# A decoder layer on one core: the top-k threshold of sparse attention found by steered counts and a max of eight instead of a bitwise search

## The chip, the core and the metric

The kernel runs on one core of one Trainium2 chip. Its engines run side by side, each with its own queue in program order: TensorE (PE, matmuls; PEld its weight loads), VectorE (DVE), ScalarE (ACT), GpSimd (POOL) and SyncE (SP, which issues all transfers here). The metric is the device time of one execution in microseconds; lower is better.

## The reference, cut to what matters

One layer on 1024 tokens of width 1024: an input norm, a joint projection, sliding-window attention (A) beside sparse attention (B), an output projection, cross-attention over 256 memory tokens, and an MLP. The change is in how B chooses its keys:

```python
dots = einsum('bqhd,bsd->bqhs', iqb, ik) * (IDX_DIM ** -0.5)   # 8 index heads of 64
score = einsum('bqh,bqhs->bqs', iwb, relu(dots))
score = where(causal, score, NEG_INF)
_, idx = lax.top_k(score, 256)        # per row; ties: the lower index wins
...                                   # attention over these 256 keys alone
```

A row with at most 256 keys (blocks 0 and 1 of 128 rows) keeps them all. So only blocks n = 2 to 7, with 384 to 1024 keys, need a choice.

## The kernel before, in words

All matmuls split fp32 operands into a high and a low part. Rows lie on the 128 partitions in eight blocks. `index_scores` (L599) leaves the scores of block n in `sc` as 128 x (n+1)*128 fp32.

The threshold of a row is its 256th largest score. It is searched bit by bit on an integer key of the score: `to_keys` (L590) turns the upper 16 bits into an ordered int16 key, and a loop at L706 does the same with the lower 16. `search` (L692) runs 15 rounds on the upper halves. After that the lower halves are masked to the rows' equal upper halves (L709 to L712), and 16 more rounds run on them. In a round each block has one look: a pass over the keys that counts those at or above a trial bound, and two 128x1 steps that set or clear the bit. Blocks 5, 4, 3 and 2 are counted on DVE (`Counter`, L649, by `count`, L583), blocks 7 and 6 on ACT as a sum of signs (`Signer`, L670). Then the key is put together as fp32 (L714 to L727), and for each block five passes of DVE (L733 to L737) turn `sc` into an additive mask: 0 for a chosen key and -1e30 for another, with a running sum that lets only the needed number of equal scores through. Sparse attention (`dsa_unit`, L838) adds that mask at L860.

Meanwhile PE works on `fill` (L490 to L550), a list of 60 units of other work: 18 projections of queries and keys (weights split by POOL, results copied by ACT at L393 and split by POOL at L395, L396), the latent keys, and the keys, values and output products of the memory tokens (`mem_k`, `mem_v`, `mem_vo`; some of their weights are split by DVE at L158 and L161, and DVE finishes values at L466). Weights come through four raw tiles (`wr`), loaded by SP at L152 and freed by the splits. Every unit is traced after the whole search:

```python
    behind["PE"] = [Pace(score_mm, 45, 1.2)]
    for unit, *args in fill:
        unit(*args)
```

A planner orders each engine's queue: by the order of tracing where it can, by its own forecast of when operands are ready where not. Attention (L884) follows, units of A and B in turn.

Of the kernel before, what the change touches and what calls it, by code (L numbers as in the profile page):

```python
# [21 lines left out]
P = 128  # L22
KT = D // P
NB = T // P
# [3 lines left out]
NEG = -1e30  # L28
ALPHA = 2.0 ** 0.25
BUCKETS = 32  # L30
NOSYNC = mybir.DependencyInfo(mybir.DependencyClass.NoSync, mybir.DependencyReason.DATA)


# [1 line left out]
def kernel(ctx: ExitStack, tc: tile.TileContext, x, mem, ln_emb_g, ln_emb_b, w_in, b_in,  # L35
# [25 lines left out]
    def f(ap):  # L61
        return ap.bitcast(F32)
# [28 lines left out]
    class Pace:  # L91

        def __init__(self, lead, start, rate):
            self.lead, self.at, self.rate = lead, start, rate
# [179 lines left out]
        ACT.activation(xin[tb], xin[tb], AF.Identity, scale=r, bias=nm)  # L274


    TW = 328
    TC = ((0, 640, 128), (128, 1280, 128), (256, 1920, 72))
    btok = p0.tile([P, TW], F32)
# [58 lines left out]
    for tb in range(NB):  # L338
        tok_cols(tb)
    bias_rows()  # L340
    st0.close()
    HALVES = ((0, 512), (512, 512))

# [8 lines left out]
    def kdup(pl, src, *names):  # L352
        kk = [place(pl, n, [P, T], F32R) for n in names]
        for hl in range(2):
            for e in range(2):
                SP.dma_start(f(kk[hl])[e * 64:e * 64 + 64], src[hl])
        return kk
# [191 lines left out]
    for at, u in zip((13, 11, 10, 9, 8, 6, 5), [(open_attention,)] + [(first_loads, i) for i in range(6)]):  # L549
        fill.insert(len(fill) - at, u)  # L550

    ik = kdup(p1, ik_d, ("ikh",), ("ikl",))
    cm = p1.tile([P, P], F32, name="cm")
    DVE.memset(cm, 0.0)
# [1 line left out]

    ring = [0]
    score_mm = []
    hi_k = {}
    HI = {7: (3, 0), 3: (7, 1024), 6: (4, 0), 4: (6, 896), 5: (2, 0), 2: (5, 768)}  # L560
    NQ = NB - 2
    cnt0, neg, flip, low, least, T_hi, base, need, t_lo = (
        p1.tile([P, NQ], F32, name=nm) for nm in ("cnt0", "neg", "flip", "low", "least", "T_hi", "base", "need", "t_lo"))

    def halves(n, which, dt=U16):
        return sc.bitcast(dt)[:, which + 2 * SCO[n]:2 * (SCO[n] + (n + 1) * P):2]

    def hi_half(n):
        mate, o = HI[n]
        if (n, mate) not in hi_k:  # L570
            hi_k[n, mate] = hi_k[mate, n] = p1.tile([P, 1536], I16, name="hi_k", tag="qs", bufs=4)
        hi_k[n] = hi_k[n, mate][:, o:o + (n + 1) * P]
        return hi_k[n]

    def col(t, n):
        return t[:, n - 2:n - 1]

    junk = {}

    def new_junk():  # L580
        junk["v"] = p1.tile([P, 1024], BF, name="junk", tag="r", bufs=3)

    def count(key, c, o, op=OP.is_ge):  # L583
        DVE.tensor_scalar(junk["v"][:, :key.shape[-1]], key, c, None, op0=op, op1=OP.add, accum_out=o)

    def to_keys(n):  # L590
        new_junk()
        count(halves(n, 1, I16), 0.0, col(cnt0, n))
        DVE.tensor_scalar(col(neg, n), col(cnt0, n), float(TOPK), -1.0, op0=OP.is_ge, op1=OP.add)
        DVE.tensor_scalar(col(flip, n), col(neg, n), 2.0, 1.0, op0=OP.mult, op1=OP.add)
        POOL.tensor_scalar(hi_half(n), halves(n, 1, I16), col(flip, n), col(neg, n), op0=OP.mult, op1=OP.add)
        DVE.tensor_scalar(col(least, n), col(neg, n), col(cnt0, n), float(TOPK), op0=OP.mult, op1=OP.add)
        DVE.tensor_scalar(col(low, n), col(neg, n), -65535.0, None, op0=OP.mult)

    def index_scores(j, qs):  # L599
        for e in range(2):  # L600
            h = 2 * j + e
            for n in (2, 4, 6, 3, 5, 7):
# [15 lines left out]
                else:  # L618
                    DVE.scalar_tensor_tensor(s, r[:, :w], iw, s, op0=OP.mult, op1=OP.add)
                if h == 7:  # L620
                    to_keys(n)

    ahead = None
    for j in range(4):
# [5 lines left out]
        ahead = (j, qs)  # L630
    index_scores(*ahead)

    SIGN = (NB - 1, NB - 2)
    lo_k = {}
    for tag, bufs, ns in (("ikh", 1, (7, 6)), ("ikl", 1, (5, 4, 3)), ("qs", 4, (2,))):
        t = p1.tile([P, sum(n + 1 for n in ns) * P], U16, name="lo_k", tag=tag, bufs=bufs)
        o = 0
        for n in ns:  # L640
            lo_k[n] = t[:, o:o + (n + 1) * P]
            o += (n + 1) * P
    new_junk()
    junk_a = p1.tile([P, 1024], BF, name="junk_a", tag="r", bufs=3)

    def srow(n):
        return sc[:, SCO[n]:SCO[n] + (n + 1) * P]

    class Counter:  # L649

        def __init__(self, n, key, least, out, bits):
            self.n, self.key, self.least, self.out, self.bits = n, key, least, out, bits
            self.c = self.small("c")
            DVE.memset(self.c, float(1 << bits - 1))

        def small(self, nm):
            return p1.tile([P, 1], F32, name=nm + str(self.n), bufs=2)

        def look(self):
            self.got = self.small("n")  # L660
            count(self.key, self.c, self.got)

        def move(self, b):
            u = self.small("u")
            DVE.tensor_scalar(u, self.got, self.least, float(1 << b), op0=OP.is_ge, op1=OP.mult)
            o = self.small("c") if b else self.out
            DVE.tensor_scalar(o, u, self.c, -float(1 << b) / 2 if b else -1.0, op0=OP.add, op1=OP.add)
            self.c = o

    class Signer(Counter):  # L670

        def __init__(self, n, key, least, out, bits):
            self.n, self.key, self.out, self.bits = n, key, out, bits
            self.c, self.least = self.small("c"), self.small("l")
            DVE.memset(self.c, 0.5 - (1 << bits - 1))
            DVE.tensor_scalar(self.least, least, -2.0, float((n + 1) * P + 1), op0=OP.mult, op1=OP.add)

        def look(self):
            self.got = self.small("n")
            ACT.activation(junk_a[:, :self.key.shape[-1]], self.key, AF.Sign, bias=self.c, accum_out=self.got)  # L680

        def move(self, b):
            u = self.small("u")
            ACT.activation(u, self.got, AF.Sign, bias=self.least)
            if b:
                o = self.small("c")
                ACT.activation(o, u, AF.Identity, scale=-float(1 << b) / 2, bias=self.c)
                self.c = o
            else:
                DVE.tensor_scalar(self.out, u, 0.5, self.c, op0=OP.mult, op1=OP.subtract)  # L690

    def search(keys, least, out, bits):  # L692
        every = [(Signer if n in SIGN else Counter)(n, keys[n], col(least, n), col(out, n), bits) for n in range(NB - 1, 1, -1)]
        last = None
        for b in range(bits - 1, -1, -1):
            for s in every:
                s.look()
                if isinstance(s, Signer):
                    s.move(b)
                    continue  # L700
                if last is not None:
                    last[0].move(last[1])
                last = s, b
        last[0].move(last[1])

    for n in range(2, NB):  # L706
        POOL.tensor_scalar(lo_k[n], halves(n, 0), col(flip, n), col(low, n), op0=OP.mult, op1=OP.add)
    search(hi_k, least, T_hi, 15)
    for n in range(NB - 1, 1, -1):  # L709
        count(hi_k[n], col(T_hi, n), col(base, n), OP.is_gt)  # L710
        DVE.scalar_tensor_tensor(lo_k[n], hi_k[n], col(T_hi, n), lo_k[n], op0=OP.is_equal, op1=OP.mult)
        DVE.tensor_scalar(col(need, n), col(base, n), -1.0, col(least, n), op0=OP.mult, op1=OP.add)  # L712
    search(lo_k, need, t_lo, 16)
    thr = p1.tile([P, NQ], I32)  # L714
    hi_i = p1.tile([P, NQ], I32)
    lo = p1.tile([P, NQ], F32)
    DVE.tensor_tensor(out=lo, in0=t_lo, in1=flip, op=OP.mult)
    DVE.tensor_tensor(out=thr, in0=lo, in1=low, op=OP.add)
    DVE.tensor_tensor(out=lo, in0=T_hi, in1=flip, op=OP.mult)
    DVE.tensor_tensor(out=lo, in0=lo, in1=neg, op=OP.add)  # L720
    DVE.tensor_scalar(hi_i, lo, 65536.0, None, op0=OP.mult)
    DVE.tensor_tensor(out=thr, in0=thr, in1=hi_i, op=OP.bitwise_or)
    ngt = p1.tile([P, NQ], F32)
    for n in range(2, NB):
        count(lo_k[n], col(t_lo, n), col(ngt, n), OP.is_gt)
    DVE.tensor_tensor(out=ngt, in0=ngt, in1=need, op=OP.subtract)
    DVE.tensor_scalar(ngt, ngt, -NEG, None, op0=OP.mult)  # L727
    for n in range(2, NB):
        w = (n + 1) * P
        s = srow(n)  # L730
        t = f(thr[:, n - 2:n - 1])
        e, pre, le = (p1.tile([P, 1024], F32, name="r", bufs=3) for _ in range(3))
        DVE.tensor_scalar(e[:, :w], s, t, -NEG, op0=OP.is_equal, op1=OP.mult)  # L733
        DVE.tensor_tensor_scan(pre[:, :w], e[:, :w], e[:, :w], ngt[:, n - 2:n - 1], OP.add, OP.bypass)
        DVE.tensor_scalar(le[:, :w], s, t, NEG, op0=OP.is_le, op1=OP.mult)
        DVE.scalar_tensor_tensor(e[:, :w], pre[:, :w], -0.5 * NEG, e[:, :w], op0=OP.is_le, op1=OP.mult)
        DVE.tensor_tensor(out=s, in0=e[:, :w], in1=le[:, :w], op=OP.add)  # L737

    behind["PE"] = [Pace(score_mm, 45, 1.2)]
    for unit, *args in fill:  # L740
        unit(*args)
    behind.clear()
    s1.close()
# [676 lines left out]
```

## Time and profile before

| | us |
|---|---|
| median of 3 runs | 1579.77 (1577.89 to 1583.2) |
| the profiled execution | 1573.87 |
| its span | 1572.0 |
| PE / DVE / POOL / ACT busy | 1449.3 / 1165.3 / 847.4 / 798.3 |
| mean granted TensorE clock | 0.967 of full |

Busy time adds up instructions, so a PE at half its clock is busy longer with the same work; the granted clock has to be read beside it. The scores are done at about 161 us from the span's start; the last mask row ends at 384.7.

### The profile page before, as it was taken

The page shows a single profiled execution, that of the slowest core. Times are in us where ns is not written, and L with a number is a line of the kernel's source. Part 1 is how long each engine was busy: PE and PEld are TensorE (multiplying, and loading weights), DVE is VectorE, ACT ScalarE, POOL GpSimd, SP SyncE. Part 2 cuts the span into 40 slices and gives each one's busy share as a digit, 9 for nine tenths or more (in the row PEclk, how much of TensorE's full clock was granted, in tenths as well). Part 3 has the DMA queues.
Part 4 walks back from the last instruction along what each step waited for, and adds up shares of the span by engine and source line. Part 5 has one row for each costly group of instructions (what it writes and reads, how often), then busy time and mean ns, then how long its engine had stood idle before and what let it go on. Part 6 is the DMA issues. An engine that isn't in the chain of part 4 may idle for free. (4 is left out here: it accounts for less than half of the span.)

```text
span 1572.0 us, 22293 instructions
## 1 busy us (share of the span) xinstructions
PE 1449.3 (92%) x7190; PEld 1208.9 (77%) x7190; DVE 1165.3 (74%) x2442; ACT 798.3 (51%) x1665; POOL 847.4 (54%) x753
## 2 busy tenths in 40 slices
PE   5989998785998999899999979999999999999887
PEld 4877776765897987688888758888888887888666
DVE  8639899969687868985263495575544799988857
ACT  6336677664787864235334154545455444444422
POOL 6213856546556555666565585645445345454745
PEclk9999998986999999999999989999999999999999
DMA  6252445873748248633322133423333934420002
GB/s 218 75 161 68 135 134 154 247 237 93 211 137 241 94 154 267 185 103 105 101 82 84 42 102 121 138 103 129 113 106 100 395 110 134 145 70 1 27 32 103
DMA packets 139907, 206.63 MB, mean 131 GB/s; under 512 B 18055, under 2 KB 83086, under 8 KB 139790
## 3 DMA queue, kind: packets, MB, share of 16 engines
q1 hardware_dynamic: 139790, 205.21, 41.4%
q8 instruction: 57, 0.93, 0.3%
q14 instruction: 60, 0.49, 0.1%
HBM read 151.66 MB, written 52.45 MB: 130 GB/s over the span
## 5 line engine op out<-in xcount | busy, mean ns | idle before, releaser
L86 PE MATMUL b<-a,wh 128*128 128x512 f32 x1072 | 300.2, 402 | 8.8 <-DVE a L1075 8.1
L161 POOL TENSOR_TENSOR wl<-wr,wh 128x512 fp32r<-128x512 f32 x158 | 228.5, 1466 | 145.8 <-ACT wh L160 137.4
L86 PE MATMUL b<-wl,wh 128*128 128x512 f32 x1192 | 278.1, 393 | 13.5 <-POOL wl L1089 13.3
L86 PEld LDWEIGHTS b<-wl,wh 128*128 128x128 f32 x1192 | 224.9, 189 | 63.9 <-POOL wl L1089 16.3
L86 PEld LDWEIGHTS b<-a,wh 128*128 128x128 f32 x1072 | 203.5, 191 | 58.2 <-issue 8.9
L1089 POOL TENSOR_TENSOR wl<-a,wl 128x512 fp32r<-128x512 f32 x44 | 92.4, 2099 | 109.0 <-ACT wl L1088 99.2
L160 ACT ACTIVATE wh<-wr 128x512 fp32r<-128x512 f32 x136 | 81.1, 627 | 128.5 <-PE b L86 46.4
L1089 POOL TENSOR_TENSOR wh<-row,wh 128x512 fp32r<-128x512 f32 x72 | 98.1, 1368 | 88.5 <-ACT wh L1088 85.2
L86 PE MATMUL fill<-xT,wh 128*128 128x512 f32 (+1 forms) x416 | 126.8, 384 | 6.8 <-ACT wt L393 6.8
L86 PE MATMUL b<-wh,a 128*128 128x512 f32 (+1 forms) x416 | 122.5, 369 | 7.6 <-DVE a L761 5.6
L86 PE MATMUL b<-a,wl 128*128 128x512 f32 x400 | 123.0, 396 | 0.0
L1088 ACT ACTIVATE wh<-a 128x512 fp32r<-128x512 f32 x80 | 50.5, 631 | 111.5 <-PE b L86 82.0
L86 PEld LDWEIGHTS fill<-xT,wh 128*128 128x128 f32 x416 | 78.5, 195 | 23.0 <-ACT wt L393 8.3
L86 PEld LDWEIGHTS b<-wh,a 128*128 128x128 f32 x416 | 76.4, 191 | 22.8 <-DVE a L761 5.9
L1282 DVE TENSOR_TENSOR xr<-xr,b 128x512 f32<-128x512 f32 x132 | 81.5, 675 | 14.1 <-PE b L86 14.1
L86 PEld LDWEIGHTS b<-a,wl 128*128 128x128 f32 x400 | 75.0, 188 | 17.4
L86 PE MATMUL fill<-xT,wl 128*128 128x512 f32 (+1 forms) x208 | 79.8, 385 | 0.0
L1100 ACT ACTIVATE lt<-lt,colst 128x512 f32<-128x512 f32 x60 | 43.2, 722 | 68.1 <-DVE lt L1207 67.3
L86 PE MATMUL b<-wl,a 128*128 128x512 f32 (+1 forms) x208 | 76.2, 369 | 1.3 <-POOL wl L161 1.3
L1207 DVE TENSOR_TENSOR lt<-b,lt 128x512 f32<-128x512 f32 x80 | 53.3, 686 | 32.1 <-PE b L86 27.5
L769 DVE TENSOR_TENSOR PT<-tr,PT 128x512 fp32r<-128x512 f32 (+3 forms) x128 | 70.6, 576 | 8.7 <-ACT PT L768 8.4
L768 ACT ACTIVATE PT<-tr 128x512 fp32r<-128x512 f32 (+3 forms) x128 | 61.4, 507 | 25.1 <-PE tr L870 11.6
(327 smaller groups left out, 3664.8 us busy)
## 6 DMA issues: line engine op xcount, KB each, us to landing
row<-in_w_up_dram SPq DMA_DIRECT2D x32, 512.0 KB, 4.3
ff_d<-lt SPq DMA_DIRECT2D x28, 512.0 KB, 3.0
a<-in_w_down_dram SPq DMA_DIRECT2D x50, 256.0 KB, 5.2
a<-ff_d SPq DMA_DIRECT2D x46, 256.0 KB, 3.5
wr<-in_xa_wkv_dram SPq DMA_DIRECT2D x32, 256.0 KB, 4.0
wr<-in_w_o_dram SPq DMA_DIRECT2D x32, 256.0 KB, 3.2
wr<-in_xa_wq_dram SPq DMA_DIRECT2D x32, 256.0 KB, 2.7
wr<-vwo_d SPq DMA_DIRECT2D x32, 256.0 KB, 2.8
```

Source lines behind the costliest of these rows:

```text
L86: i = PE.matmul(o, a, b, start=start, stop=stop)
L160: ACT.activation(hs, raw, AF.Copy)
L161: lo[i % len(lo)].tensor_tensor(out=ls, in0=raw, in1=f(hs), op=OP.subtract)
L768: ACT.activation(PT[0], pt, AF.Copy)
L769: DVE.tensor_tensor(out=PT[1], in0=pt, in1=f(PT[0]), op=OP.subtract)
L1088: ACT.activation(hl[:, 0], raw, AF.Copy)
L1089: return lo.tensor_tensor(out=hl[:, 1], in0=raw, in1=f(hl[:, 0]), op=OP.subtract)
L1100: ACT.activation(c, src, AF.Relu, bias=colst[:, C_UP + col:C_UP + col + 1])
L1207: DVE.tensor_tensor(out=o, in0=a, in1=b, op=op)
L1282: DVE.tensor_tensor(out=xs, in0=xs, in1=p, op=op)
```

## The change

The integer keys and both searches go. In their place:

* `normal_bounds` (at the end of the first stage) works out, for each row's number of keys, where a normal distribution has its 251.5th largest value, and the slope there.
* When a block's scores are done, mean and deviation of the first 256 to 512 of them (`bn_stats`, `bn_aggr`, a power on POOL) give a first bound and a step per count.
* Eight rounds (`PULL`) of one look per block: the count of scores at or above the bound, compared with 251.5, moves the bound. The looks read the fp32 scores themselves; blocks 7 and 6 stay on ACT.
* A last count gives how many of the 256 are still below the bound (`need`). The scores at or above it are pushed down by 2^100, and a max-8 gives the eight largest of the rest: the `need`-th of them is the threshold.
* If any row has a `need` outside 1 to 8, all six blocks are settled by the old bitwise search, now on DVE alone and one step after another, behind a branch. The flag is gathered by a matmul of one column and read into a register of DVE.
* The mask rows keep their five passes. They are now traced, with the branch ahead of them, after the first 26 units of `fill` (`CUT`) and ahead of the other 34.

```diff
+PULL = (1.0, 0.8, 0.6, 0.9, 0.5, 0.3, 0.6, 0.25)
+WANT = TOPK - 4.5
...
+            w = min(512, n * P)
+            st, mv, sd = (self.own[:, a:b] for a, b in ((0, 6), (6, 8), (8, 9)))
+            DVE.bn_stats(st, srow(n)[:, :w])
+            DVE.bn_aggr(mv, st)
+            POOL.tensor_tensor(out=sd, in0=mv[:, 1:2], in1=half_up, op=OP.pow)
+            self.begin(mv, sd)
...
+        def begin(self, mv, sd):
+            self.c, g, self.rate = self.small("c"), self.own[:, 9:10], self.own[:, 12:20]
+            DVE.tensor_scalar(self.c, sd, col(zc, self.n), mv[:, 0:1], op0=OP.mult, op1=OP.add)
+            DVE.tensor_scalar(g, sd, col(gp, self.n), None, op0=OP.mult)
+            DVE.tensor_scalar(self.rate, pull, g, None, op0=OP.mult)
+        def look(self):
+            self.got = self.small("n")
+            s = srow(self.n)
+            DVE.tensor_scalar(junk["v"][:, :s.shape[-1]], s, self.c, None, op0=OP.is_ge, op1=OP.add, accum_out=self.got)
+
+        def move(self, i):
+            u, o = self.small("u"), self.small("c") if i < len(PULL) - 1 else col(bound, self.n)
+            DVE.tensor_scalar(u, self.got, WANT, self.rate[:, i:i + 1], op0=OP.subtract, op1=OP.mult)
+            DVE.tensor_scalar(o, u, self.c, None, op0=OP.add)
+            self.c = o
+
...
+    class Signer(Counter):
...
+        def look(self):
+            self.got = self.small("n")
+            s = srow(self.n)
+            ACT.activation(junk["a"][:, :s.shape[-1]], s, AF.Sign, bias=self.c, accum_out=self.got)
...
-                    to_keys(n)
+                    every[n] = (Signer if n in SIGN else Counter)(n)
...
-    search(hi_k, least, T_hi, 15)
...
-    search(lo_k, need, t_lo, 16)
...
+    for i in range(len(PULL)):
+        for n in range(NB - 1, 1, -1):
+            s = every[n]
+            s.look()
+            if n in SIGN:
+                s.move(i)
+                continue
+            if last is not None:
+                last[0].move(last[1])
...
+    for n in ORDER:
+        over[n] = p1.tile([P, 1024], BF, name="over", tag="qs", bufs=4)
+        DVE.tensor_scalar(over[n][:, :(n + 1) * P], srow(n), col(bound, n), None, op0=OP.is_ge, op1=OP.add, accum_out=col(base, n))
+    DVE.tensor_scalar(need, base, -1.0, float(TOPK), op0=OP.mult, op1=OP.add)
...
+    DVE.tensor_scalar(odd1, odd1, 16.0, None, op0=OP.is_gt)
+    ones = p1.tile([P, 1], F32, name="ones")
+    DVE.memset(ones, 1.0)
+    po = psum.tile([P, 512], F32, name="odd_rows", tag="mm", bufs=2)
+    PE.matmul(po[:1, :1], odd1, ones, start=True, stop=True)
+    some = p1.tile([1, 1], I32, name="some")
+    DVE.tensor_scalar(some, po[:1, :1], 1.0, None, op0=OP.min)
+    for i, n in enumerate(ORDER):
+        w = (n + 1) * P
+        v = p1.tile([P, 1024], F32, name="v", tag=("ikh", "ikl")[i % 2], bufs=1)
+        DVE.scalar_tensor_tensor(v[:, :w], over[n][:, :w], LAST, srow(n), op0=OP.mult, op1=OP.add)
+        DVE.max(m8[:, n - 2], v[:, :w])
...
+    def by_bits(key, most, least, o, bits, a, go, scratch):
+        go(DVE.memset(a[0], float(1 << bits - 1)))
         for b in range(bits - 1, -1, -1):
+            go(DVE.tensor_scalar(scratch, key, a[0], None, op0=OP.is_ge, op1=OP.add, accum_out=a[1]))
+            go(DVE.tensor_scalar(a[1], a[1], least, float(1 << b), op0=OP.is_ge, op1=OP.mult))
+            go(DVE.tensor_scalar(a[0], a[1], a[0], -float(1 << b) / 2 if b else -1.0, op0=OP.add, op1=OP.add))
...
+    def settle_all():
+        rest = nc.values_load(some, [mybir.EngineType.DVE], min_val=0, max_val=1)
+        with tc.tile_critical():
+            with nc.If(rest > 0):
+                for n in range(2, NB):
+                    settle(n)
...
-    for unit, *args in fill:
+    for unit, *args in fill[:CUT]:
+        unit(*args)
+    settle_all()
+    mask_rows()
+    for unit, *args in fill[CUT:]:
         unit(*args)
```

`settle(n)` makes the keys of one block, calls `by_bits` with 15 and with 16 bits, and puts the threshold together; each of its instructions waits for the one before. In `before`, the round loop and the classes are the removed ones named above.

## Rows read from the trace of the kernel before

**Rows 1.** The page, parts 1 and 2: busy time by engine; granted clock in 40 slices.

```profile
PE 1449.3 (92%) x7190; PEld 1208.9 (77%) x7190; DVE 1165.3 (74%) x2442; ACT 798.3 (51%) x1665; POOL 847.4 (54%) x753
PEclk9999998986999999999999989999999999999999
```

**Rows 2.** Windows: stretch, length, busy PE, PEld, DVE, ACT, POOL, clock, DMA share, GB/s.

```profile
160.00:230.00 70.00, 68.10 (x305) 55.28 (x304) 65.79 (x261) 53.71 (x136) 52.37 (x55) 1.00 0.50 139
230.00:354.00 124.00, 100.47 (x553) 86.05 (x551) 111.42 (x346) 83.80 (x198) 65.00 (x57) 0.88 0.67 210
354.00:400.00 46.00, 30.14 (x169) 26.97 (x170) 43.66 (x111) 21.74 (x65) 26.52 (x31) 0.74 0.34 86
400.00:1572.00 1172.00, 1118.73 (x5476) 928.17 (x5474) 829.30 (x1460) 559.62 (x1110) 644.24 (x546) 0.98 0.39 125
```

**Rows 3.** Waits of PE in 230 to 354: who, for whom, us, times, longest.

```profile
PE fill L86 <- DVE wl L161: 10.4, 7, 2.6
PE fill L86 <- ACT wt L393: 4.9, 1, 4.9
...
PE fill L86 <- DVE wh L158: 2.1, 3, 0.8
```

**Rows 4.** Timeline of DVE: start, us, operation; one round of four looks.

```profile
306.46 0.99 DVE L584 TENSOR_SCALAR_CACHE_REDUCE junk<-lo_k,c 128x768 bf16<-128x768 uint16 x1
...
307.39 0.20 DVE L665 TENSOR_SCALAR u<-n,need 128x1 f32<-128x1 f32 x1
307.52 0.20 DVE L667 TENSOR_SCALAR c<-u,c 128x1 f32<-128x1 f32 x1
...
310.37 1.00 DVE L584 TENSOR_SCALAR_CACHE_REDUCE junk<-lo_k,c 128x768 bf16<-128x768 uint16 x1
```

**Rows 5.** Waits of the SP queue in 200 to 360.

```profile
SPq L152 <- DVE wl L161: 24.1, 7, 5.5
```

**Rows 6.** Timeline of ACT: two looks of one block, and the second search's first.

```profile
205.71 1.06 ACT L680 ACTIVATE junk_a<-hi_k,c 128x896 bf16<-128x896 int16 x1
...
208.61 1.06 ACT L680 ACTIVATE junk_a<-hi_k,c 128x896 bf16<-128x896 int16 x1
...
234.74 1.15 ACT L680 ACTIVATE junk_a<-lo_k,c 128x1024 bf16<-128x1024 uint16 x1 [10.76 <-DVE lo_k L711]
```

**Rows 7.** Timeline of DVE: the last scores, and mask rows.

```profile
158.99 1.80 DVE L619 SCALAR_TENSOR_TENSOR sc<-r,iwt,sc 128x1024 f32<-128x1024 f32 x1
...
346.22 0.42 DVE L733 TENSOR_SCALAR r<-sc,thr 128x384 f32<-128x384 f32 x1
...
363.87 0.60 DVE L735 TENSOR_SCALAR r<-sc,thr 128x768 f32<-128x768 f32 x1
...
383.42 1.30 DVE L737 TENSOR_TENSOR sc<-r 128x1024 f32<-128x1024 f32 x1
```

**Rows 8.** Waits of PE in 354 to 400, the longest.

```profile
PE mm L86 <- DVE PT L769: 7.3, 1, 7.3
```

**Rows 9.** Groups of DVE by line in 346 to 385: busy us, mean ns, idle before.

```profile
L734 DVE TENSOR_TENSOR_SCAN r<-r,ngt 128x384 f32<-128x384 f32 (+5 forms) x6 | 10.2, 1704 | 0.1
L736 DVE SCALAR_TENSOR_TENSOR r<-r 128x384 f32<-128x384 f32 (+5 forms) x6 | 5.6, 940 | 0.0
L737 DVE TENSOR_TENSOR sc<-r 128x384 f32<-128x384 f32 (+5 forms) x6 | 5.5, 914 | 0.1
L733 DVE TENSOR_SCALAR r<-sc,thr 128x384 f32<-128x384 f32 (+5 forms) x6 | 5.0, 830 | 0.0
L735 DVE TENSOR_SCALAR r<-sc,thr 128x384 f32<-128x384 f32 (+5 forms) x6 | 4.5, 756 | 0.0
```

**Rows 10.** Line L584's instructions in 160 to 400: ns min/median/max, start, forms.

```profile
L584 DVE TENSOR_SCALAR_CACHE_REDUCE junk<-hi_k,T_hi x6: 603/936/1279, 232.2 to 240.4; 128x1024 bf16<-128x1024 int16 x1, 128x896 bf16<-128x896 int16 x1, 128x768 bf16<-128x768 int16 x1, 128x640 bf16<-128x640 int16 x1
```

**Rows 11.** Groups of DVE by form in 0 to 170: bn_stats of 512 columns.

```profile
L268 DVE BATCH_NORM_STATS2 bst<-wt 128x6 f32<-128x512 f32 x10 | 6.2, 663 | 2.5 <-DMA wt<-in_x_dram 2.5
```

**Rows 12.** The page, part 3: the instruction queue; packets, MB, share.

```profile
q8 instruction: 57, 0.93, 0.3%
```

More of the change, by code (lines that the diff above doesn't have):

```diff
@@ L30 @@
 BUCKETS = 32
+PULL = (1.0, 0.8, 0.6, 0.9, 0.5, 0.3, 0.6, 0.25)
+WANT = TOPK - 4.5
+LAST = -2.0 ** 100
 NOSYNC = mybir.DependencyInfo(mybir.DependencyClass.NoSync, mybir.DependencyReason.DATA)
@@ L340 @@
     bias_rows()
+    normal_bounds()
     st0.close()
@@ L550 @@
         fill.insert(len(fill) - at, u)
+    CUT = 26
     ik = kdup(p1, ik_d, ("ikh",), ("ikl",))
@@ L558, with srow @@
     score_mm = []
[L559 to L563, printed above, removed]
+    SIGN = (NB - 1, NB - 2)
+    bound, base, need, thr, ngt = (p1.tile([P, NQ], F32, name=nm) for nm in ("bound", "base", "need", "thr", "ngt"))
+    def srow(n):
+        return sc[:, SCO[n]:SCO[n] + (n + 1) * P]
@@ L565, in halves @@
     def halves(n, which, dt=U16):
         return sc.bitcast(dt)[:, which + 2 * SCO[n]:2 * (SCO[n] + (n + 1) * P):2]
[L568 to L573, printed above, removed]
     def col(t, n):
         return t[:, n - 2:n - 1]
-    junk = {}
-    def new_junk():
-        junk["v"] = p1.tile([P, 1024], BF, name="junk", tag="r", bufs=3)
@@ L583, in count, with __init__, small @@
[L583 to L597, printed above, removed]
+    class Counter:
+        def __init__(self, n):
+            self.n = n
+            self.own = p1.tile([P, 20], F32, name="own%d" % n)
+            self.way = p1.tile([P, 6], F32, name="way%d" % n)
+            self.turn = [0, 0, 0]
+            w = min(512, n * P)
[4 more added lines that the diff above has]
+            self.begin(mv, sd)
+        def small(self, nm):
+            k = "cnu".index(nm)
+            self.turn[k] += 1
+            i = 2 * k + self.turn[k] % 2
+            return self.way[:, i:i + 1]
+        def begin(self, mv, sd):
[12 more added lines that the diff above has]
+            self.c = o
@@ new lines, with begin, move @@
+    class Signer(Counter):
+        def begin(self, mv, sd):
+            self.c, g, self.rate = self.small("c"), self.own[:, 9:10], self.own[:, 12:20]
+            self.even = self.own[:, 10:11]
+            DVE.memset(self.even, (self.n + 1) * P - 2 * WANT)
+            DVE.tensor_scalar(self.c, sd, col(zn, self.n), mv[:, 0:1], op0=OP.mult, op1=OP.subtract)
+            DVE.tensor_scalar(g, sd, col(gn, self.n), None, op0=OP.mult)
+            DVE.tensor_scalar(self.rate, pull, g, None, op0=OP.mult)
+        def look(self):
+            self.got = self.small("n")
+            s = srow(self.n)
+            ACT.activation(junk["a"][:, :s.shape[-1]], s, AF.Sign, bias=self.c, accum_out=self.got)
+        def move(self, i):
+            u = self.small("u")
+            ACT.activation(u, self.got, AF.Identity, bias=self.even)
+            if i < len(PULL) - 1:
+                o = self.small("c")
+                ACT.activation(o, u, AF.Identity, scale=self.rate[:, i:i + 1], bias=self.c)
+                self.c = o
+            else:
+                v = self.own[:, 11:12]
+                DVE.tensor_scalar(v, u, self.rate[:, i:i + 1], self.c, op0=OP.mult, op1=OP.add)
+                DVE.tensor_scalar(col(bound, self.n), v, -1.0, None, op0=OP.mult)
@@ L599, in index_scores @@
+    junk, every = {}, {}
     def index_scores(j, qs):
@@ L631 @@
     index_scores(*ahead)
[L635 to L690, printed above, removed]
@@ L692, in search @@
-    def search(keys, least, out, bits):
-        every = [(Signer if n in SIGN else Counter)(n, keys[n], col(least, n), col(out, n), bits) for n in range(NB - 1, 1, -1)]
-        last = None
-        for b in range(bits - 1, -1, -1):
[L696 to L704, printed above, removed]
@@ L706 @@
-    for n in range(2, NB):
-        POOL.tensor_scalar(lo_k[n], halves(n, 0), col(flip, n), col(low, n), op0=OP.mult, op1=OP.add)
-    search(hi_k, least, T_hi, 15)
[L709 to L712, printed above, removed]
-    search(lo_k, need, t_lo, 16)
@@ L714 @@
[L714 to L728, printed above, removed]
-        w = (n + 1) * P
[L730 to L737, printed above, removed]
@@ L739 @@
-    behind["PE"] = [Pace(score_mm, 45, 1.2)]
-    for unit, *args in fill:
+    for k in ("v", "a"):
+        junk[k] = p1.tile([P, 1024], BF, name="junk", tag="r", bufs=3)
+    last = None
+    for i in range(len(PULL)):
[7 more added lines that the diff above has]
+                last[0].move(last[1])
+            last = s, i
+    last[0].move(last[1])
@@ new lines @@
+    m8 = p1.tile([P, NQ, 8], F32, name="m8")
+    ORDER = (2, 3, 4, 5, 6, 7)
+    over = {}
+    for n in ORDER:
+        over[n] = p1.tile([P, 1024], BF, name="over", tag="qs", bufs=4)
+        DVE.tensor_scalar(over[n][:, :(n + 1) * P], srow(n), col(bound, n), None, op0=OP.is_ge, op1=OP.add, accum_out=col(base, n))
+    DVE.tensor_scalar(need, base, -1.0, float(TOPK), op0=OP.mult, op1=OP.add)
+    odd, odd1 = p1.tile([P, NQ], F32, name="odd"), p1.tile([P, 1], F32, name="odd1")
+    DVE.tensor_scalar(odd, need, -4.5, None, op0=OP.add)
@@ new lines @@
+    DVE.tensor_tensor(out=odd, in0=odd, in1=odd, op=OP.mult)
+    DVE.tensor_reduce(out=odd1, in_=odd, op=OP.max, axis=AX.X)
+    DVE.tensor_scalar(odd1, odd1, 16.0, None, op0=OP.is_gt)
[5 more added lines that the diff above has]
+    DVE.tensor_scalar(some, po[:1, :1], 1.0, None, op0=OP.min)
@@ new lines, with each @@
+    for i, n in enumerate(ORDER):
[3 more added lines that the diff above has]
+        DVE.max(m8[:, n - 2], v[:, :w])
+    sel = p1.tile([P, NQ, 8], F32, name="sel")
+    def each(t):
+        return t.rearrange("p (n o) -> p n o", o=1).to_broadcast([P, NQ, 8])
+    DVE.tensor_tensor(out=sel, in0=turn8.to_broadcast([P, NQ, 8]), in1=each(need), op=OP.is_equal)
@@ new lines @@
+    DVE.tensor_tensor(out=sel, in0=sel, in1=m8, op=OP.mult)
+    DVE.tensor_reduce(out=thr, in_=sel, op=OP.add, axis=AX.X)
+    DVE.tensor_tensor(out=sel, in0=m8, in1=each(thr), op=OP.is_gt)
+    DVE.tensor_reduce(out=ngt, in_=sel, op=OP.add, axis=AX.X)
+    DVE.tensor_tensor(out=ngt, in0=ngt, in1=need, op=OP.subtract)
+    def by_bits(key, most, least, o, bits, a, go, scratch):
+        go(DVE.memset(a[0], float(1 << bits - 1)))
+        for b in range(bits - 1, -1, -1):
+            go(DVE.tensor_scalar(scratch, key, a[0], None, op0=OP.is_ge, op1=OP.add, accum_out=a[1]))
+            go(DVE.tensor_scalar(a[1], a[1], least, float(1 << b), op0=OP.is_ge, op1=OP.mult))
+            go(DVE.tensor_scalar(a[0], a[1], a[0], -float(1 << b) / 2 if b else -1.0, op0=OP.add, op1=OP.add))
+        go(DVE.tensor_copy(o, a[0]))
+        go(DVE.tensor_scalar(scratch, key, o, None, op0=OP.is_gt, op1=OP.add, accum_out=most))
@@ new lines, in settle_all, with mask_rows @@
+    def settle_all():
[4 more added lines that the diff above has]
+                    settle(n)
+    def mask_rows():
+        DVE.tensor_scalar(ngt, ngt, -NEG, None, op0=OP.mult)
+        for i, n in enumerate(ORDER):
+            w = (n + 1) * P
+            s, t = srow(n), col(thr, n)
+            e, le = (p1.tile([P, 1024], F32, name="r", bufs=3) for _ in range(2))
+            pre = p1.tile([P, 1024], F32, name="pre", tag=("ikh", "ikl")[i % 2], bufs=1)
+            DVE.tensor_scalar(e[:, :w], s, t, -NEG, op0=OP.is_equal, op1=OP.mult)
+            DVE.tensor_tensor_scan(pre[:, :w], e[:, :w], e[:, :w], ngt[:, n - 2:n - 1], OP.add, OP.bypass)
+            DVE.tensor_scalar(le[:, :w], s, t, NEG, op0=OP.is_le, op1=OP.mult)
+            DVE.scalar_tensor_tensor(e[:, :w], pre[:, :w], -0.5 * NEG, e[:, :w], op0=OP.is_le, op1=OP.mult)
+            DVE.tensor_tensor(out=s, in0=e[:, :w], in1=le[:, :w], op=OP.add)
```

64 lines of the change are left out of this document (added).

## Prediction

> **What bounds the kernel now.** I read the page first, then the windows by stage, then TensorE's waits, then the queues that those waits point at. Over the whole run TensorE (PE) is the bound: 92% busy against 74% of VectorE (DVE), with a granted clock near full, lowest in slices 7, 9 and 10 [rows 1]. So an edit to the top-k search, which is DVE and ScalarE (ACT) work, is worth only what PE loses around it.
>
> The windows give that loss. PE busy times granted clock is work at full rate: 68.1 us of 70 in 160 to 230, but 100.47 x 0.88 = 88.4 of 124 in 230 to 354, and 30.14 x 0.74 = 22.3 of 46 in 354 to 400; after 400 it is 1118.73 x 0.98 = 1096 of 1172, or 93.5% [rows 2]. So 1.9 + 35.6 + 23.7 = 61.2 us are lost while the search runs. That is the ceiling of any gain; at the 93.5% of the later stages the 178.8 us of work would take 191 of the 240, and 49 would be saved.
>
> Who causes it: in 230 to 354 PE is idle 23.5 us. DVE splits of weights that come late (wl 10.4, wh 2.1) and ACT's copy of a projection (4.9) are 17.4 of it [rows 3]. The splits are late since DVE does nothing but count: a round of four looks lasts from 306.46 to 310.37, 3.91 us, without a gap [rows 4]. Late splits also free the raw tiles late, and the loads' own queue stands 24.1 us behind them [rows 5]. The 4.9 us is a different thing: ACT stood 10.76 us in front of its first look of the second search, until DVE had masked the low halves, and the projection's copy was queued behind it [rows 6]. In 354 to 400 attention could run but its DVE steps stand behind mask rows that go from 346.22 to 384.7 [rows 7]; the longest single wait, 7.3 us for PT, ends with the last of them [rows 8].
>
> **The change part by part.** *Rounds.* 15 + 16 = 31 rounds become 8. A look has the same shape, but reads fp32 scores where it read 16-bit keys. The trace has no fp32 look: a 768-wide fp32 compare without the sum took 0.60 us [rows 7], the 16-bit look with the sum 0.99 [rows 4]. I take 0.99, as the sum is the thing they share. 8 x 3.91 = 31.3 us instead of 31 x 3.91 = 121.2: 90 us of DVE go. Of a round the looks are 3.91 less eight small steps at 0.13 from start to start, 2.9 us. At 0.60 for 0.99 they would give some 9 us more over eight rounds; were they twice as long, 23 us come back. ACT's pair of rounds takes 2.90 us (from 205.71 to 208.61) [rows 6], below 3.91, so ACT still keeps up, and loses 23 x 2.9 = 67 us of load. The second search goes, and its 10.76 us wait with it.
>
> [...]
>
> *Keys and estimate.* The sign counts, the four small steps and the twelve POOL conversions go; six bn_stats (663 ns each [rows 11]) with an aggregate and three small steps come, and six POOL powers of one column. On DVE these are even within 2 us. The 128x6 set-up of the bounds is some 15 small steps on DVE and as many on POOL, after the token projections. DVE has room there, and PE waits for none of it: 0, at worst 2.
>
> *End of the search.* Gone: two sets of six counts (936 ns in the middle, 5.6 us a set [rows 10]), six products, the putting together of the key: about 22 us. New: six counts at the bound, 5.6; six products that lift the chosen ones out, priced like the 5.6 us of L736 [rows 9]; six max-8, which no row shows: between the 5.5 of L737 and the 10.2 of the scan [rows 9], taken as 5.6, one pass over the data; some 14 small steps at 0.20 [rows 4], 3; one matmul there and back, 1. Together 21 us, so even. An error of 5 us either way is covered as long as PE has fill work.
>
> *Branch.* No row shows one. DVE must read the flag into a register and jump over 6 x (31 x 4 + 20), some 860 instructions. The nearest row is the instruction queue: 57 packets in 0.3% of 16 x 1572 us, 1.3 us each [rows 12]. I take 3 us, from 0 to 10, on DVE alone. Behind it in DVE's queue stand the mask rows and later splits. The units before the cut are mostly projections, split by POOL and copied by ACT, so PE does not need DVE there. If the section held the other engines too, that cover is gone (rival B).
>
> [...]
>
> *Mask rows and cut.* The mask's five passes are unchanged, 5.0 + 10.2 + 4.5 + 5.6 + 5.5 = 31 us [rows 9]. Tracing them after the first 26 fill units moves them past those units in every queue. The scores end at 160.8 [rows 7]. Then 31 (rounds) + 21 + 3 + 31, and about 12 of splits between them, ends the mask near 260 instead of 384.7. The masks are ready before attention, so its start then depends on the fill and on its own loads.
>
> **The sum.** In 230 to 354: 17.4 us of the idle time go, 75% of what is listed by cause, and I let the clock loss (100.47 - 88.4 = 12.1) follow it, 9.1: 26.5. Off this: the search still fills DVE until 260, while the memory units that need its splits begin near 240, so about 20 us of their some 108 still see a full DVE: -5. In 354 to 400: at 93.5% the work takes 23.9 instead of 46, 22 less; I keep 5 for an attention whose loads, due earlier, have not all landed: 17. Together 38.5. The profiled execution took 1573.87 (its span 1572.0), and 5.9 less than the median of 1579.77. 1573.9 - 38.5 = 1535.4; on the median's footing 1579.8 - 38.5 = 1541.3. I forecast 1541 us.
>
> **The rivals.** *A, the branch is taken: slower.* It decides from one row among 768 on: each must end with 1 to 8 of the top 256 still below its bound, else all six blocks are settled bit by bit. By hand, a step multiplies the miss by 1 - pull x density ratio; the eight pulls leave 4.5% of a first miss where scores are half as dense as the normal says, 19% where 0.3 times, and next to nothing at once or twice. A miss of 30 becomes 1.4 or 6; only the thin tails and ties fail. Price: a bit over all blocks is 5.6 for counts [rows 10] plus 6 x 2 small steps at 0.20 [rows 4], 8.0 us, times 31 is 248, and conversions and ends, six more passes over the six blocks and some 80 small steps, are 34 + 16: some 300 us on DVE. It holds DVE from about 225 to 525; PE runs dry near 255, when the memory units want DVE splits. 1580 + 270 - 20 = about 1830. For it: the scores are sums of eight rectified products, not normal. Against: the damping above.
>
> *B, the critical section ties PE down.* Its matmul stands in PE's queue, and if DVE comes later than was planned, or the section stops all engines, PE waits at the cut, then restarts at a lower clock with its loads not running ahead. From 10 to 20 us of the gain go: about 1557. For it: an atomic piece of code in the midst of the fill; against: only DVE reads the flag.
>
> *C, the fill is bound by its loads and POOL's splits.* Then 230 to 354 gives little and only attention's 17 us come, with some 5 more: about 1558. For it: DMA share 0.67 over the stretch [rows 2]; against: the queue waits for DVE.
>
> *D, the fill and attention overlap well*: the 49 us of the ceiling, or some more: 1527.
>
> **How the numbers follow.** Forecast 45%, its own range 1532 to 1550; B 20%, C 13%, D 8%, A 8%; no change within 0.3% (4.7 us, about what a measurement of this kernel can tell) 4%, slower through delays on DVE that PE feels, without the branch, 2%. Faster: 0.45 + 0.20 + 0.13 + 0.08 = 0.86; same 0.04; slower 0.10. The range 1515 to 1577 takes in B, C, D and the unknown costs of looks and max-8, and leaves out A and the ends.
>
> **What would show it.** Right: eight looks of some 1.0 us per block, masks done near 260, no 10.76 us hole on ACT, PE's window from 230 on above 90% at full clock, attention some 40 us earlier and everything after it shifted unchanged. Wrong: some 860 more DVE instructions before the mask (A); PE idle at the matmul of the flag (B); PE waiting for POOL or loads for as long as it waited for DVE (C); fp32 looks near 2 us.

## The result and the profile after

The changed kernel takes 1596.55 us (median of 4 runs, 1594.72 to 1597.92) against 1579.91 for the kernel before (4 runs, 1577.89 to 1583.2): 1.0097 of its time, 95% interval 1.0077 to 1.0117. It is 16.6 us slower; the forecast was 38.5 us faster. The profiled execution took 1597.32 us, its span 1595.0.

The page of the changed kernel, parts 1 and 2, answers to [rows 1]: busy time of each engine, then PE's busy tenths, granted clock and DMA share in 40 slices of 39.9 us.

```profile
PE 1429.9 (90%) x7192; PEld 1199.5 (75%) x7192; DVE 1082.8 (68%) x2061; ACT 734.2 (46%) x1483; POOL 843.1 (53%) x763
...
PE   4987077998999999899999979999999999999897
...
PEclk9999578999999999999999999999999999999999
DMA  6261024489568637733322224333323933320002
```

DVE lost 82 us of work and ACT 64, as meant. But PE has a slice with nothing in it, the fifth, and there the transfers are at 0 too. The windows of the changed kernel (length, busy PE, PEld, DVE, ACT, POOL, clock, DMA share, GB/s) answer to [rows 2]:

```profile
140.00:160.00 20.00, 12.15 (x50) 7.38 (x48) 20.00 (x32) 12.88 (x29) 3.13 (x3) 0.87 0.00 1
160.00:230.00 70.00, 19.93 (x75) 16.00 (x76) 58.94 (x197) 25.81 (x64) 9.43 (x11) 0.60 0.05 13
230.00:354.00 124.00, 113.64 (x559) 94.52 (x557) 49.97 (x42) 26.32 (x43) 89.11 (x76) 0.96 0.58 164
354.00:400.00 46.00, 39.68 (x251) 33.43 (x252) 7.92 (x13) 23.25 (x44) 25.87 (x22) 1.00 0.93 309
400.00:1595.00 1195.00, 1135.89 (x5681) 955.62 (x5679) 851.77 (x1548) 580.56 (x1175) 657.28 (x580) 0.98 0.40 127
```

In the kernel before, 140 to 160 reads:

```profile
140.00:160.00 20.00, 20.00 (x94) 16.68 (x94) 19.90 (x43) 11.63 (x25) 5.86 (x7) 1.00 0.15 40
```

The prediction takes busy time times the mean clock of a stretch as the work done in it. Here that misleads: the 0.60 of 160 to 230 is mostly the clock of a PE that waits (0.50 from 160 to 210), so 19.93 x 0.60 = 12.0 is too little. (In the stretches that the prediction itself summed this changes under 1 us: 87.7 for 88.4, 22.8 for 22.3.) Summed over windows of 1 us, each with its own clock, PE did this work at full rate, in us:

| | 140 to 160 | 160 to 230 | 230 to 354 | 354 to 400 |
|---|---|---|---|---|
| before | 20.0 | 68.1 | 87.7 | 22.8 |
| after | 12.2 | 16.8 | 111.0 | 39.7 |

By 230 the changed kernel is 59 us of work behind, and behind 230 it gains 40 of them back. The 19 that are missing at 400 take 20 at the rate of the stage after it (94%); the span grew by 23.0. Such sums are good to some us only: over the whole run they give 1411.8 for the kernel before and 1402.0 for this one. So the whole loss lies ahead of 230, where before almost nothing was lost; behind 230 the changed kernel is better than before, as meant.

PE's waits in 140 to 354 (who, for whom, us, times, longest), and PE's timeline around the longest:

```profile
PE odd_rows L751 <- DVE odd L747: 57.3, 1, 57.3
PE tr L482 <- DVE fb L485: 9.5, 1, 9.5
```

```profile
152.34 0.39 PE L91 MATMUL lg<-ikl,qs 128*128 128x512 f32 x1
210.07 0.19 PE L751 MATMUL odd_rows<-ones,odd 128*1 128x1 f32 x2 [57.34 <-DVE odd L747]
210.19 1.22 PE L91 MATMUL fill<-xT,wh 128*128 128x512 f32 x2
```

The product of the flag, 1x1, stands in PE's queue right behind the last score product, and waits there until DVE has the flag, near the end of the search. No fill product comes before it: all of the fill that PE was to do beside the search stands behind it. The fill's own machinery stops with it, as the longest single waits of the SP queue (86.0) and of POOL (57.4) over the whole run show:

```profile
SPq L441 <- POOL wt L439: 114.6, 18, 86.0
```

```profile
POOL wt L438 <- ACT wt L436: 76.6, 7, 57.4
```

The steps of DVE came out near their prices. Its timeline (start, us, operation): two looks of block 5 a round apart, the flag, the end of the selection, the first step behind the branch, the last mask row.

```profile
181.93 1.01 DVE L648 TENSOR_SCALAR_CACHE_REDUCE junk<-sc,way 128x768 bf16<-128x768 f32 x1
...
186.01 1.01 DVE L648 TENSOR_SCALAR_CACHE_REDUCE junk<-sc,way 128x768 bf16<-128x768 f32 x1
...
209.87 0.14 DVE L747 TENSOR_SCALAR odd<-odd 128x1 f32<-128x1 f32 x1
210.29 0.14 DVE L753 TENSOR_SCALAR some<-odd_rows 1x1 int32<-1x1 f32 x1
...
211.80 0.17 DVE L767 TENSOR_TENSOR ngt<-ngt,need 128x6 f32<-128x6 f32 x1 [0.77 <-DVE ngt L766]
221.95 0.17 DVE L824 TENSOR_SCALAR ngt<-ngt 128x6 f32<-128x6 f32 x1 [9.99 <-DVEq L818]
...
258.61 2.27 DVE L834 TENSOR_TENSOR sc<-r 128x1024 f32<-128x1024 f32 x1
```

An fp32 look takes 1.01 us where the 16-bit one took 0.99 [rows 4]; the mask ends at 260.9; the branch is not taken (nothing of the 31 bits runs), but DVE stands 9.99 us at it. DVE's groups by line in 140 to 262 (busy us, mean ns) give the max-8 and the dearest mask passes:

```profile
L831 DVE TENSOR_TENSOR_SCAN pre<-r,ngt 128x384 f32<-128x384 f32 (+5 forms) x6 | 12.0, 2014 | 0.0
L834 DVE TENSOR_TENSOR sc<-r 128x384 f32<-128x384 f32 (+5 forms) x6 | 10.6, 1762 | 0.0
...
L758 DVE MAX8 m<-v 128x8 f32<-128x384 f32 (+5 forms) x6 | 5.3, 892 | 0.0
```

### The profile page after: what moved, and what is told of

Its sections match the earlier page's. It is cut to its first block, busy times and chain, and to the rows that moved or that the text cites. A ratio compares the mean times of both kernels' runs of the same rounds, so it can differ in the third digit from the quotient of the medians.

```text
span 1595.0 us, 21766 instructions
## 1 busy us (share of the span) xinstructions
PE 1429.9 (90%) x7192; PEld 1199.5 (75%) x7192; DVE 1082.8 (68%) x2061; ACT 734.2 (46%) x1483; POOL 843.1 (53%) x763
## 5 line engine op out<-in xcount | busy, mean ns | idle before, releaser
L91 PE MATMUL b<-a,wh 128*128 128x512 f32 x1072 | 292.5, 394 | 10.0 <-DVE a L1176 8.1
L91 PE MATMUL b<-wl,wh 128*128 128x512 f32 x1192 | 282.3, 397 | 13.6 <-POOL wl L1190 11.3
```

Source lines behind the costliest of these rows:

```text
L91: i = PE.matmul(o, a, b, start=start, stop=stop)
```

## The experiments

Three theories of why the flag's product stands ahead of the fill. **The bank:** its tile is taken from PSUM tag "mm" (2 buffers), and so are the first 24 products of the fill (`fill_bank`, L409):

```
    def fill_bank():
        nfill[0] += 1
        tag = ("mm", "lg", "tr")[nfill[0] % 3] if nfill[0] > NFIRST else "mm"
        return psum.tile([P, 512], F32, name="fill", tag=tag, bufs=2 if tag == "mm" else 3)
```

By this theory buffers of a tag are handed out in the order in which the code is traced; the flag is traced ahead of the fill, so the fill's tiles of that tag come behind its product, and PE's order with them. (With two buffers one fill product could still have passed it; none did, and why the planner let none pass no run shows.) **The order of tracing** alone, whatever the tag. **The section as a fence:** the critical section or the branch holds PE.

*The flag in another bank.*

```
-    po = psum.tile([P, 512], F32, name="odd_rows", tag="mm", bufs=2)
+    po = psum.tile([P, 512], F32, name="odd_rows", tag="lg", bufs=3)
```

> Only the PSUM tag of the flag's tile is changed, from mm (2 banks, which the first 24 fill products share) to lg (3 banks, which they do not use). Theory 1, banks: PSUM tiles of a tag are handed out in the order of tracing, so no fill product could have a bank before the flag's tile had come and gone, and all of them stood behind a matmul that waits for the end of the search. Then PE's 57.3 us wait goes to under 3 us, and the time falls by 50 to 60 us, to 1536 to 1547. Theory 2, order of tracing: the matmul stands ahead because it is traced ahead of the fill. Then nothing changes: 1590 to 1600. Theory 3, the critical section: what is traced behind the search is held by the section with the branch. Then nothing changes either.

Measured: 1545.12 us (4 runs, 1541.99 to 1547.73), 0.9767 of the kernel before [0.9726, 0.9809]. PE's timeline shows the fill between the scores again:

```profile
156.56 0.63 PE L91 MATMUL fill<-xT,wh 128*128 128x512 f32 x2
157.02 0.28 PE L91 MATMUL lg<-ikh,qs 128*128 128x256 f32 x1
...
158.20 0.63 PE L91 MATMUL fill<-xT,wh 128*128 128x512 f32 x2
```

Its windows, columns as above:

```profile
160.00:230.00 70.00, 69.84 (x308) 55.66 (x308) 62.67 (x191) 36.18 (x81) 51.98 (x53) 1.00 0.52 143
230.00:300.00 70.00, 54.38 (x290) 47.84 (x290) 52.72 (x49) 14.66 (x25) 42.74 (x32) 0.85 0.57 161
300.00:354.00 54.00, 46.82 (x297) 39.77 (x296) 10.22 (x25) 27.13 (x56) 27.87 (x25) 0.97 0.91 291
354.00:400.00 46.00, 40.46 (x277) 36.55 (x277) 35.00 (x131) 33.65 (x91) 28.81 (x50) 0.96 0.60 171
```

PE is full from 160 to 230. One word of the source turns +16.6 us into -34.1 (against 1579.17, the median beside it).

*The flag later in the trace, in the old bank.* The six lines from `ones` to `some` are moved behind the 26 fill units:

```
     for unit, *args in fill[:CUT]:
         unit(*args)
+    ones = p1.tile([P, 1], F32, name="ones")
...
+    po = psum.tile([P, 512], F32, name="odd_rows", tag="mm", bufs=2)
+    PE.matmul(po[:1, :1], odd1, ones, start=True, stop=True)
...
     settle_all()
```

> The flag's tile stays in mm, but the matmul and the read of its result are traced after the first 26 fill units, just before the branch. Theory 1 (banks): the 26 units get their banks first, so this gives the same as the other tag, 1536 to 1550. Theory 2 (order of tracing): the same, 1536 to 1550. Theory 3 (critical section): 1590 to 1600, PE still idle for over 50 us.

Measured: 1545.52 us (1541.9 to 1551.81), 0.9787 [0.9743, 0.9832]. It fits both the bank and the order of tracing; only the two together tell: with another bank the early product did no harm, so the order of tracing matters only within a tag.

*No product at all.*

```
...
-    po = psum.tile([P, 512], F32, name="odd_rows", tag="mm", bufs=2)
-    PE.matmul(po[:1, :1], odd1, ones, start=True, stop=True)
...
+    DVE.memset(some, 0)
```

> The flag is a constant zero: the counts are not gathered, the branch stays and is still read and jumped over. This leaves out the fallback. Theories 1 and 2: 1535 to 1548, and within 3 us of the kernel with the flag in its own banks, since one matmul of one column costs nothing. Theory 3: 1590 to 1600.

Measured: 1548.23 us (1540.45 to 1549.52), 0.9793 [0.9754, 0.9832]. The median lies a hair outside what was expected (1535 to 1548, within 3 us of 1545.1), with runs that spread over 9 us. The product itself costs nothing that can be seen.

*The product, without read, section and branch.*

```
-    settle_all()
     mask_rows()
```

> The register read, the section and the branch are taken out, the matmul stays where it was, in mm. This leaves out the fallback. Theory 3 (critical section): 1530 to 1548. Theories 1 and 2: PE still waits some 57 us at the matmul; only the 10 us in which DVE stood at the branch go, and as PE has its fill by then, some 0 to 9 us come of it: 1587 to 1597.

Measured: 1588.34 us (10 runs, 1584.11 to 1593.66), 1.0049 [1.0028, 1.007]. The section is gone and PE's wait is not:

```profile
PE odd_rows L751 <- DVE odd L747: 57.4, 1, 57.4
```

The fence falls as the cause; read, section and branch are worth 8 us beside the wait.

*The old search with such a product.* Nothing of the change; where the upper halves' search of the kernel before ends, ahead of the fill:

```
     search(hi_k, least, T_hi, 15)
+    odd1, ones = p1.tile([P, 1], F32, name="odd1"), p1.tile([P, 1], F32, name="ones")
+    DVE.tensor_reduce(out=odd1, in_=T_hi, op=OP.max, axis=AX.X)
+    DVE.memset(ones, 1.0)
+    po = psum.tile([P, 512], F32, name="mm", tag="mm", bufs=2)
+    PE.matmul(po[:1, :1], odd1, ones, start=True, stop=True)
+    some = p1.tile([1, 1], I32, name="some")
+    DVE.tensor_scalar(some, po[:1, :1], 1.0, None, op0=OP.min)
```

> The kernel before with nothing of the new search: a 1x1 fp32 product of a maximum of T_hi, into a bank of the tag 'mm', traced where the upper halves' search ends, ahead of the fill. Theory (a tile of this tag, traced ahead of the fill, holds every fill product until DVE's search comes to it): TensorE stands from the last score, near 160, to the end of that search, near 232, some 70 us, of which nine tenths are lost as with the changed kernel (57 us idle cost 51): 1630 to 1655. Rival (the loss belongs to the new search, its section or its branch, and a small product costs what it takes): within 5 us of 1580.

Measured: 1641.61 us (1640.41 to 1644.12), 1.0399 [1.038, 1.0418]: 62.9 us slower than before. PE's longest wait:

```profile
PE mm L713 <- DVE odd L710: 76.8, 1, 76.8
```

The loss is made in the old kernel by those lines alone, at 82% of the wait (I had said nine tenths). The wait is not the only thing that moved: PE also waits 19.2 us once for a DVE split (`wh`), where the kernel before had 2.1 in three [rows 3].

*What is left: the hole at the branch.* With the flag in "lg", DVE's first step behind the branch shows `11.43 <-DMA qb_d<-wt`; the copy named has nothing to do with `ngt`, it only ended last. Without read, section and branch:

```
-    settle_all()
     mask_rows()
```

> The kernel with the flag's product in the 'lg' bank (1545 us), and without the register read, the critical section and the branch; it leaves out the bit-by-bit fallback. DVE then has no 11.4 us hole before the mask rows. If the hole is on the path (the mask rows, and behind them DVE's first splits for the memory projection, come 11 us earlier): the 9.2 us that TensorE waits for 'wh' goes and the time falls by 7 to 12 us, to about 1536. If TensorE's work before 250 us covers it, or a later wait (loads) takes its place: within 3 us of 1545.

Measured: 1538.72 us (5 runs, 1537.54 to 1540.92), 0.9746 [0.9731, 0.9761]: 6.4 us below 1545.1, just short of the 7 to 12 expected if the hole is on the path. But the way there was not the one expected: PE's wait for `wh` fell only from 9.2 to 6.1, and that for DVE's `wl` rose from 2.2 to 6.7. DVE's order changed too: the mask passes start at 224.7, ahead of the flag's return, where they had started at 239.4. The intervals of the two overlap, but on the same chip with the same runs of before the program of the first experiment took 1544.29 (below, the later cut), 5.6 more, and the pair with the old bank differs by 8: read, section and branch together cost some 6.

*The read alone*: in the critical section, `pass` in place of the branch and its body.

> The flag's product in the 'lg' bank; DVE still reads the flag into a register, in an empty critical section, but the branch and its body are left out (so the bit-by-bit fallback is left out). If the 9 to 11 us hole on DVE ahead of the mask rows is the jump over some 680 DVE instructions: no hole over 3 us there, time as without the whole block, 1539. If it is the read of the flag into the register or the section: the hole stays at 8 us or more, time near 1545.

Measured: 1540.75 us (1538.25 to 1541.75), 0.9744 [0.971, 0.9779]. DVE's timeline shows no hole behind the flag:

```profile
235.14 0.14 DVE L753 TENSOR_SCALAR some<-odd_rows 1x1 int32<-1x1 f32 x1
...
236.74 0.69 DVE L832 TENSOR_TENSOR sc<-r 128x512 f32<-128x512 f32 x1
```

(the 1.40 us between are a mask pass). The hole comes with the branch, not with the read. (As without the section, the first mask passes rank ahead of the flag here.)

*A short body*: the branch jumps over one block's settling instead of six.

```
-                for n in range(2, NB):
+                for n in range(2, 3):
```

> The flag's product in the 'lg' bank, with branch and section, but a body that settles one block instead of six (the fallback is left out for five blocks). If the hole grows with the length of what is jumped over: 2 to 4 us instead of 11.4. If any jump costs one stall, whatever its length: 8 to 12 us, time near 1545. Where the hole is short the time should be between 1539 and 1543.

Measured: 1541.63 us (1540.92 to 1543.9), 0.9746 [0.9712, 0.9781].

```profile
235.61 0.31 DVE L824 TENSOR_SCALAR ngt<-ngt 128x6 f32<-128x6 f32 x1 [8.23 <-PE fill L91]
```

A sixth of the body, and the hole is 8.23 us; with the whole body the runs show 8.59 to 11.73. So most of it is there with the short body too; whether the length adds up to 3 us these single profiles don't settle. The time fits the other case, 1539 to 1543: with a hole of 8.23 us this kernel takes only 0.9 us more than the one without a branch, timed beside it, less than the spread of either. So the hole's length is not its price in time; how much of it reaches the time stays open.

*Splits without DVE.* The memory projection's weights are split by ACT and POOL alone:

```
-... (ACT, DVE) if both else (ACT,), (POOL, DVE) if both else (POOL,))
+... (ACT,), (POOL,))
```

> The flag's product in the 'lg' bank, and the memory projection's weights split by ACT and POOL alone, so that TensorE waits for nothing that stands in DVE's queue behind the branch and the mask rows. Theory (what is left of the loss is that wait on DVE, 9.2 + 2.2 us of PE idle and the lower clock after it): 5 to 15 us below 1545, about 1536, and no PE wait on 'wh' before 300. Rival (POOL, then with all the low halves, at 1.3 to 2.6 us each, or the loads become the bound): the wait turns into one for POOL's 'wl' or for DMA, time 1540 to 1555.

Measured: 1541.98 us (1535.77 to 1544.44), 0.9759 [0.9737, 0.978], not to be told from the first experiment. PE's waits in 140 to 420:

```profile
PE fill L91 <- POOL wl L166: 8.5, 6, 2.9
PE fill L91 <- ACT wh L165: 7.9, 4, 2.6
```

The wait on DVE turned into waits on POOL and ACT, as the rival said.

*A later cut* (`CUT = 36`).

> The flag's product in the 'lg' bank, and 36 instead of 26 fill units traced ahead of the branch and the mask rows, so that DVE's splits for the first four memory projections rank before them. Theory (the splits were late because they rank behind branch and masks): the 9.2 us PE wait on 'wh' goes, masks end later by the ten to twenty microseconds of those splits and of the wait for their loads; attention starts near 350, so it hardly feels that: about 1537. Rival (the DVE queue then waits for loads ahead of the branch, and the masks come too late for attention): 1545 to 1560, with DVE idle before the branch and PE waiting near 350.

Measured: 1544.29 us (1539.86 to 1547.01), 0.9773 [0.9755, 0.9792]. It tells nothing of the splits: the program built from it is, instruction for instruction on every engine, that of the first experiment. Presumably the planner puts the masks and splits by due time, so that the place of the cut between 26 and 36 doesn't matter; no run shows that. So it is a second timing of that kernel: 1545.1 and 1544.3.

The best kernel that keeps the fallback is thus the change with the flag's tile in another bank, about 1545; the one with ACT and POOL splitting and the one with the flag traced later are its equals.

## Why the prediction was wrong

*The step that failed* is the flag's product, "one matmul there and back, 1", in the end of the search. On DVE that holds (from 209.87 to 210.29). On PE it was never priced: nothing that stands behind the product in PE's queue ran from the time the queue reached it to the time its operand was there, 152.7 to 210.1. The diff and the kernel showed what was needed: the tag "mm" on the added tile, traced ahead of the fill, and `fill_bank`, whose first 24 products take the same tag. The statement "PE does not need DVE there" was true of the fill units and false of the product ahead of them.

*Rival B* named the place ("Its matmul stands in PE's queue") and gave it 20%, but for other reasons (a late DVE, a section that stops all engines) and at 10 to 20 us. The wait is 57.3 and costs 51 (1596.6 against 1545.1). For a price the profile before had what it took: from the last score to the end of the search PE is full [rows 2], and in the trace with matmuls of fill units alone, so a product that waits for that end idles PE for the whole length of the search, by the prediction's own terms 31 + 21 = 52 us.

*The rest of the change*, read from the first experiment, is worth 34.1 us against 38.5 forecast. The total is near, its parts are not:
- *354 to 400:* 17 forecast; by windows of 1 us 38.9 us of work against 22.8, which is 17 us at 94%. Right.
- *230 to 354:* 26.5 - 5 = 21.5 forecast; 93.3 us of work against 87.7, only 6 us at 94%. The 17.4 us of idle time that were to go did not: PE is idle 22.8 us here (124 less 54.38 and 46.82), against 23.5 before; what came is a better clock. This term of the sum was mis-sized. PE's waits in 150 to 420 of that kernel say why:

```profile
PE fill L91 <- DVE wh L163: 9.2, 1, 9.2
PE fill L91 <- POOL wl L166: 7.6, 10, 4.1
```

  The many waits for DVE's splits [rows 3] became one of 9.2 and one of 2.2, the first for a split queued among the mask rows, behind the branch, and others for POOL; the clock fell to 0.85 in the stretch with that wait, and from 300 on the transfers are at 0.91. Rival C had the size of this stretch right; of its causes, POOL shows 7.6 us here and takes DVE's place only where DVE splits nothing (8.5, beside 7.9 for ACT).
- *160 to 230:* 1.7 us of work, 2 us of time, none forecast. Together some 25 us by these sums, where the spans differ by 27.5, which is as near as such sums come. The medians differ by 34.1, since the profiled execution of before lay 5.3 below its median (1573.87 to 1579.17) and this one 1.5 above.

*Looks* at the price of the 16-bit ones: right, 1.01 us against 0.99. The 23 us that looks of twice the length would have taken back did not come. *Max-8* 5.3 against 5.6 taken. *Search over* 53.9 us after the last score step (158.1 to 212.0) against 31 + 21 = 52: right, but with POOL idle beside it (busy 1.76 us in 160 to 210). In the first experiment, where the fill runs beside the search as the prediction had it, the search ends 65.6 us after the last score step (161.2 to 226.8), and the mask at 279.2. *ACT's 10.76 us hole* [rows 6] went with the second search. *Mask near 260:* 260.9 in the changed kernel, but by other terms: the branch took 9.99 instead of 3 (the end of its range) and the five passes 40.3 instead of 31, while the 12 us of splits between them did not come, as the fill stood.

*The branch.* The 3 us taken, from 0 to 10, were an estimate from the time of an instruction packet [rows 12]; DVE stood 8.23 to 11.73 us in seven profiles. What it waits for there no run shows. The cover that I counted on holds only in part: without read, section and branch the time falls by 5.6 to 8.2 us in three pairs of kernels, without the branch alone by 4.4 (1545.12 to 1540.75), but the short branch costs 0.9.

## What to carry to other kernels

A small product that carries a flag through TensorE is priced by what stands behind it in the queue while its operand is late, not by its own length (here 0.19 us of its own, 57.3 of wait, 51 in the time): ask of each instruction added to the bound engine when its operand comes, and who is behind it. As this kernel is scheduled, a PSUM tag (a pool of buffers that matmuls write) acted as a queue of its own: the tile traced early with a late writer held the fill's first tiles of its tag for 57.3 us, and in another tag held none, so a late, small result belongs in a tag that the covering work doesn't use. When a change that thins an engine out makes a kernel slower, look first for a slice in which the bound engine is empty; here one row of its waits held the whole answer.

## What the runs showed of the hardware

- TensorE's granted clock stood at 0.50 from 160 to 210, while it waited, at 0.61 in the 8 us after, and at 1.00 from 218 to 226. Three fill products (two with `wh`, one with `wl`) took 1.28 us from start to start at 0.50 (from 211.63 to 212.91) and 0.70 at 1.00 (from 217.24 to 217.94). The windows of the changed kernel, columns as above:

```profile
160.00:210.00 50.00, 0.00 (x0) 0.00 (x0) 49.89 (x181) 24.43 (x62) 1.76 (x4) 0.50 0.00 0
210.00:218.00 8.00, 7.93 (x24) 6.31 (x25) 1.04 (x7) 0.00 (x0) 0.00 (x0) 0.61 0.00 0
218.00:226.00 8.00, 8.00 (x36) 6.46 (x35) 4.05 (x7) 1.38 (x2) 3.67 (x4) 1.00 0.37 95
```

  So the wait cost some 3 us more than its length there (0.39 of 8), which the denser work behind it more than gave back (111.0 us of work in 230 to 354, against 93.3 in the first experiment): 57.3 us of waiting cost 51, and 76.8 cost 62.9.
- At a branch that skips its body DVE stood 8.23 us with 114 instructions of the body to jump over (one block, counted from the code), and 8.59 to 11.73 in six profiles with 684 (six blocks); with the flag read into a register and no branch the profile shows no hole (0.11 us from the start of the flag's step to that of the next).
- The mask passes and POOL's splits were slow side by side. In the changed kernel L834, the same operation as L737 before, takes 1762 ns in the mean against 914 [rows 9]. POOL's groups in 222 to 262, against 1554 ns for the same split in 346 to 385 before:

```profile
L166 POOL TENSOR_TENSOR wl<-wr,wh 128x512 fp32r<-128x512 f32 x6 | 12.0, 2007 | 0.0
L439 POOL TENSOR_TENSOR wt<-wt 128x512 fp32r<-128x512 f32 x5 | 10.7, 2134 | 0.3
```

  In the first experiment POOL splits beside the end of the search, where in the changed kernel it is idle, and two steps of 128x6 take 1.26 and 1.25 us, each ending within 0.03 us of the end of an instruction of POOL (214.27 and 219.60):

```profile
213.03 1.26 DVE L741 TENSOR_SCALAR need<-base 128x6 f32<-128x6 f32 x1
218.38 1.25 DVE L745 TENSOR_TENSOR odd<-odd 128x6 f32<-128x6 f32 x1
```

```profile
212.38 1.89 POOL L439 TENSOR_TENSOR wt<-wt 128x512 fp32r<-128x512 f32 x1
216.18 3.42 POOL L166 TENSOR_TENSOR wl<-wr,wh 128x512 fp32r<-128x512 f32 x2
```

  In the profiles of the read alone and of the short body the same two take 1.26 and 1.25 us too, in the changed kernel 0.17 us each. The looks, which also write a sum, do not change (804 ns in the mean against 809), nor does the max-8 (883 against 892). That these steps and the mask passes are slow because they wait for POOL is the author's inference from these ends; no run shows it by itself.
